# A decoder block in split fp32: the two high products of k, q, u and up become one product of 512 columns, their halves added afterwards, with PSUM handed out in single banks

## Chip, core, metric

One core of a Trainium2 chip runs the whole block in one launch. The metric is the device time of that launch in microseconds (us); the kernel before takes 1664.67 us, the median of 3 runs (1663.89 to 1665.68).

## What is computed

One layer over 256 tokens, width 2048, all in float32. Cut to the parts that matter here:

```python
h = rmsnorm(x, ln_mix)
z = h @ w_in                       # columns: u, v of the gate | q, k, v | two gates
y_a = (gelu(u) * (W_s layernorm(gelu(v)) + b)) @ w_proj_a
y_b = causal_attention(q, k, v, bias) @ w_proj_b          # 16 heads of 128
x = x + (sigmoid(g_a) * y_a + sigmoid(g_b) * y_b) @ w_out
h = rmsnorm(x, ln_mlp)
x = x + square(relu(h @ w_up)) @ w_down                   # hidden width 8192
out = rmsnorm(x, ln_final)
```

## The kernel before

Every large product has both factors split exactly into a high and a low part of type float32r, w = hi + lo and a = ah + al, and three of the four part products are summed in PSUM: ah·hi, al·hi, ah·lo.

**Weights** (`WeightStream`) come in tiles of 512 rows by 512 columns. `load` issues the DMA (raw tile, 4 buffers), `split` makes the parts: ScalarE (ACT) copies raw to `whi` (L72), VectorE (DVE) subtracts to get `wlo` (L73), 3 buffers each. `get` runs the splits two tiles ahead of the products. A *chunk* is 512 output columns over all 2048 rows, that is four weight tiles, each of four blocks kk of 128 rows.

**Products** take one of two forms. `rows` (v, the gates, the projections, w_down) has the activations as the stationary operand of 128 x 128 and 512 columns of weights moving: 24 products of 512 columns per tile. `cols` (kt, qt, u, up) gives the transposed result: the stationary operand is one of four blocks n of 128 weight columns, and 256 tokens of activations move. Per kk it runs (hi, ah) for n = 0 to 3, then (hi, al), then (lo, ah): 12 products of 256 columns, 48 per tile, 192 per chunk. There are 28 such chunks: kt, qt and u four each (kt and qt in turn, c = 0 to 3), up 16 (b = 0 to 3, c = 0 to 3). Up chunks are named up*b*_*c*.

**PSUM.** The results of `rows` and `cols` share the tag `mm` with two buffers of two banks each: one chunk fills one buffer while the chunk before is read out of the other. A chunk of `cols` holds n = 0, 1 in one bank and n = 2, 3 in the other. Its readers after the chunk are two DVE instructions of 512 columns (`scale_cols` L332, u L432, up L525), for up followed by two squares on ACT each (L527, L528) and a subtraction on DVE (L529), which make the high and low part of the hidden activations.

**Order.** The code is written in program order, and side tasks (attention heads, gating, transposes) are issued between weight tiles by `tick`. The framework then schedules every engine's instructions by its own model of durations, so that the order on an engine isn't always that of the code; on the chip an engine runs its list in that order and waits on semaphores.

Of the kernel before, what the change touches and what calls it, by code (L numbers as in the profile page):

```python
# [12 lines left out]
F32 = mybir.dt.float32  # L13
F32R = mybir.dt.float32r
# [4 lines left out]
P = 128  # L19
# [68 lines left out]
def block_kernel(ctx, tc, x, x_t, ln_mix, w_in, v_gain, w_sp, b_sp, w_pa, w_pb, w_out, rel_bias,  # L88
# [41 lines left out]

    def rows(acts, name):
        """[tokens, CH] = acts.T @ W over 2048 rows, both token tiles."""
        ps = psum.tile([P, NT, CH], F32, tag="mm", name=name, bufs=2)
        for i in range(KT // KG):
            hi, lo = stream.get()
            for kk in range(KG):
                k = i * KG + kk
                ah, al = acts(k)
                for t in range(NT):
                    s = slice(t * P, (t + 1) * P)  # L140
                    nc.tensor.matmul(ps[:, t], ah[:, s], hi[:, kk], start=k == 0, stop=False)  # L141
                    nc.tensor.matmul(ps[:, t], ah[:, s], lo[:, kk], start=False, stop=False)  # L142
                    nc.tensor.matmul(ps[:, t], al[:, s], hi[:, kk], start=False, stop=k == KT - 1)  # L143
            if i < KT // KG - 1:
                tick()
        return ps

    def cols(acts, name):
        """[CH as 4 x 128, tokens] = W.T @ acts over 2048 rows."""
        ps = psum.tile([P, CH // P, T], F32, tag="mm", name=name, bufs=2)  # L150
        for i in range(KT // KG):
            hi, lo = stream.get()
            for kk in range(KG):
                k = i * KG + kk
                ah, al = acts(k)
# [491 lines left out]
```

## Time and profile before

| what | value |
|---|---|
| median of 3 runs | 1664.67 us |
| profiled execution, its span from the first to the last instruction | 1662.5 us |
| TensorE (PE) busy | 1651.6 us, 99% of the span |
| weight loads (PEld) | 1483.7 us, 89%, beside PE |
| DVE, ACT busy | 850.9 us (51%), 688.8 us (41%) |
| read from HBM | 311.5 MB |

The profiled execution has no time of its own beside its span; the span is 2.2 us under the median of the runs, and this remainder is taken as what lies around the span. The page lists busy time by engine, the chain of work that ended last, and groups of instructions by source line. Products on PE overlap in the records (the end of one is modelled), so their rate has to be read from start to start in the timeline and not from their durations.

### The profile page before, as it was taken

The page shows a single profiled execution, that of the slowest core. Times are in us where ns is not written, and L with a number is a line of the kernel's source. Part 1 is how long each engine was busy: PE and PEld are TensorE (multiplying, and loading weights), DVE is VectorE, ACT ScalarE, POOL GpSimd, SP SyncE. Part 2 cuts the span into 40 slices and gives each one's busy share as a digit, 9 for nine tenths or more (in the row PEclk, how much of TensorE's full clock was granted, in tenths as well). Part 3 has the DMA queues.
Part 4 walks back from the last instruction along what each step waited for, and adds up shares of the span by engine and source line. Part 5 has one row for each costly group of instructions (what it writes and reads, how often), then busy time and mean ns, then how long its engine had stood idle before and what let it go on. Part 6 is the DMA issues. An engine that isn't in the chain of part 4 may idle for free.

```text
span 1662.5 us, 22670 instructions
## 1 busy us (share of the span) xinstructions
PE 1651.6 (99%) x9988; PEld 1483.7 (89%) x9988; DVE 850.9 (51%) x726; ACT 688.8 (41%) x614; POOL 4.3 (0%) x11
## 2 busy tenths in 40 slices
PE   9999999999999999999999999999999999999997
PEld 9899999888888899888888999889988998899986
DVE  7545544544445555544555555444545455445554
ACT  7444343443334443434444444334443443334432
POOL 0000000000000000000000000000000000000000
PEclk9999999999999999999999999999999999999999
DMA  9855444465555554555465554555555555555551
GB/s 317 254 193 187 165 178 170 159 223 185 200 192 189 192 199 169 184 191 202 178 234 189 210 178 178 202 189 191 178 186 194 190 190 178 201 181 186 190 183 74
DMA packets 51762, 317.16 MB, mean 191 GB/s; under 512 B 5664, under 2 KB 10832, under 8 KB 14928
## 3 DMA queue, kind: packets, MB, share of 16 engines
q1 hardware_dynamic: 51632, 315.71, 53.9%
q8 instruction: 78, 1.28, 0.3%
q14 instruction: 20, 0.16, 0.0%
q0 software_dynamic: 32, 0.01, 0.0%
HBM read 311.50 MB, written 4.19 MB: 190 GB/s over the span
## 4 chain that ended last, share of the span: by engine, by line
PE 99%; DMA 0%; DVE 0%; ACT 0%; issue 0%; DVEq 0%; POOL 0%; POOLq 0%; ACTq 0%
PE up L158 22%; PE dn L142 7%; PE dn L143 7%; PE dn L141 7%; PE kt L158 6%; PE qt L158 6%; PE u L158 6%; PE v L142 2%; PE wo L143 2%; PE ga L143 2%; PE gb L141 2%; PE wo L141 2%; PE ga L141 2%; PE wo L142 2%; PE pa L141 2%; PE v L141 2%
## 5 line engine op out<-in xcount | busy, mean ns | idle before, releaser
L73 DVE TENSOR_TENSOR wlo<-wraw,whi 128x2048 fp32r<-128x2048 f32 (+2 forms) x297 | 658.9, 2219 | 644.8 <-ACT whi L72 644.8
L72 ACT ACTIVATE whi<-wraw 128x2048 fp32r<-128x2048 f32 (+2 forms) x297 | 551.5, 1858 | 832.6 <-PE up L158 188.9
L141 PE MATMUL dn<-whi,hh 128*128 128x512 f32 x480 | 186.8, 389 | 0.0
L142 PE MATMUL dn<-wlo,hh 128*128 128x512 f32 x480 | 186.8, 389 | 0.0
L143 PE MATMUL dn<-whi,hl 128*128 128x512 f32 x480 | 186.7, 389 | 0.0
L158 PE MATMUL up<-h2h,whi 128*128 128x256 f32 x1024 | 164.7, 283 | 0.0
L158 PE MATMUL up<-h2l,whi 128*128 128x256 f32 x1024 | 164.6, 283 | 0.0
L158 PE MATMUL up<-h2h,wlo 128*128 128x256 f32 x1024 | 164.6, 283 | 0.0
L158 PEld LDWEIGHTS up<-h2h,whi 128*128 128x128 f32 x1024 | 141.5, 192 | 0.3
L158 PEld LDWEIGHTS up<-h2h,wlo 128*128 128x128 f32 x1024 | 141.3, 192 | 0.0
L158 PEld LDWEIGHTS up<-h2l,whi 128*128 128x128 f32 x1024 | 141.3, 192 | 0.0
L143 PEld LDWEIGHTS dn<-whi,hl 128*128 128x128 f32 x480 | 90.1, 188 | 18.7
L141 PEld LDWEIGHTS dn<-whi,hh 128*128 128x128 f32 x480 | 90.1, 188 | 18.6
L142 PEld LDWEIGHTS dn<-wlo,hh 128*128 128x128 f32 x480 | 90.1, 188 | 18.6
L141 PE MATMUL gb<-whi,hh 128*128 128x512 f32 x128 | 50.6, 395 | 0.0
L141 PE MATMUL wo<-whi,mh 128*128 128x512 f32 x128 | 50.6, 395 | 0.0
L141 PE MATMUL ga<-whi,hh 128*128 128x512 f32 x128 | 50.4, 394 | 0.0
L141 PE MATMUL v<-whi,hh 128*128 128x512 f32 x128 | 50.0, 391 | 0.0
L141 PE MATMUL pa<-whi,ah 128*128 128x512 f32 x128 | 50.0, 391 | 0.0
L143 PE MATMUL wo<-whi,ml 128*128 128x512 f32 x128 | 50.0, 390 | 0.0
L142 PE MATMUL v<-wlo,hh 128*128 128x512 f32 x128 | 50.0, 390 | 0.0
L143 PE MATMUL ga<-whi,hl 128*128 128x512 f32 x128 | 49.9, 390 | 0.0
(180 smaller groups left out, 2394.8 us busy)
## 6 DMA issues: line engine op xcount, KB each, us to landing
wraw<-in_w_in SPq DMA_DIRECT2D x108, 1024.0 KB, 4.8
wraw<-in_w_up SPq DMA_DIRECT2D x64, 1024.0 KB, 4.8
wraw<-in_w_down SPq DMA_DIRECT2D x64, 1024.0 KB, 4.8
wraw<-in_w_pb SPq DMA_DIRECT2D x16, 1024.0 KB, 4.8
wraw<-in_w_pa SPq DMA_DIRECT2D x16, 1024.0 KB, 4.8
wraw<-in_w_out SPq DMA_DIRECT2D x16, 1024.0 KB, 4.8
wraw<-in_w_in SPq DMA_DIRECT2D x8, 256.0 KB, 4.7
wraw<-in_w_in SPq DMA_DIRECT2D x4, 512.0 KB, 7.5
```

The source lines that it names most:

```text
L72: self.nc.scalar.activation(hi[:, s], t[:, s], AF.Copy)
L73: self.nc.vector.tensor_tensor(lo[:, s], t[:, s], hi[:, s].bitcast(F32), ALU.subtract)
L141: nc.tensor.matmul(ps[:, t], ah[:, s], hi[:, kk], start=k == 0, stop=False)
L142: nc.tensor.matmul(ps[:, t], ah[:, s], lo[:, kk], start=False, stop=False)
L143: nc.tensor.matmul(ps[:, t], al[:, s], hi[:, kk], start=False, stop=k == KT - 1)
L158: nc.tensor.matmul(ps[:, n], w[:, kk, n * P : (n + 1) * P], a, start=k == 0 and j == 0 and n % 2 == 0, stop=k == KT - 1 and j == 2, skip_g ...
```

## The change

In `cols` the high weights meet both activation parts in one product: the activations are now stored as [k][2][256], high and low side by side, and the product of the block n of `hi` with these 512 columns gives ah·hi in the first half of a bank and al·hi in the second. The low weights meet the high activations in a product of 256 columns into the first half. A block n then has a PSUM bank of its own, and the result is the sum of the two halves: `fold` copies the second half out on ACT and adds the first half on DVE. The tag `mm` has four buffers of one bank: a chunk of `cols` takes all four, `rows` takes two. In a chunk's last weight tile the products run block by block (`order`), so that the first bank is complete before the last. Scaling by the norm, which DVE did while reading PSUM, is an instruction of its own on SBUF for kt and qt (1024 columns), u (512) and up (256). All pairs of activation tiles become one tile of twice the size; docstrings and comments go.

```diff
+    def order(i, n):
+        if i == KT // KG - 1:
+            return [(kk, b) for b in range(n) for kk in range(KG)]
+        return [(kk, b) for kk in range(KG) for b in range(n)]
...
     def rows(acts, name):
-        ps = psum.tile([P, NT, CH], F32, tag="mm", name=name, bufs=2)
+        ps = [psum.tile([P, CH], F32, tag="mm", name=f"{name}t{t}", bufs=4) for t in range(NT)]
         for i in range(KT // KG):
             hi, lo = stream.get()
-            for kk in range(KG):
+            for kk, t in order(i, NT):
...
-    def cols(acts, name):
-        ps = psum.tile([P, CH // P, T], F32, tag="mm", name=name, bufs=2)
+    def cols(acts, name, finish):
+        ps = [psum.tile([P, 2, T], F32, tag="mm", name=f"{name}n{n}", bufs=4) for n in range(CH // P)]
         for i in range(KT // KG):
             hi, lo = stream.get()
-            for kk in range(KG):
+            for kk, n in order(i, CH // P):
                 k = i * KG + kk
-                ah, al = acts(k)
-                for j, (w, a) in enumerate(((hi, ah), (hi, al), (lo, ah))):
-                    for n in range(CH // P):
-                        nc.tensor.matmul(ps[:, n], w[:, kk, n * P : (n + 1) * P], a,
-                                         start=k == 0 and j == 0 and n % 2 == 0,
-                                         stop=k == KT - 1 and j == 2, skip_group_check=True)
+                a, s = acts(k), slice(n * P, (n + 1) * P)
+                nc.tensor.matmul(ps[n], hi[:, kk, s], a, start=k == 0, stop=False, skip_group_check=True)
+                nc.tensor.matmul(ps[n][:, 0], lo[:, kk, s], a[:, 0], start=False, stop=k == KT - 1,
+                                 skip_group_check=True)
...
-        return ps
+        for n in range(CH // P):
+            finish(n, ps[n])
+
+    def fold(dst, ps):
+        nc.scalar.activation(dst, ps[:, 1], AF.Copy)
+        nc.vector.tensor_tensor(dst, ps[:, 0], dst, ALU.add)
...
+        def scale(dst):
+            nc.vector.tensor_tensor(dst, dst, rb[1][:, None, :].to_broadcast([P, 4, T]), ALU.mult)
+        def summed(name):
             dst = at.tile([P, 4, T], F32, tag=name[:2], name=name, bufs=2)
+            cols(hacts, name, lambda n, ps: fold(dst[:, n], ps))
             return dst
         for c in range(4):
-            ps = cols(hacts, f"kt{c}")
-            kt = scale_cols(ps, f"kt{c}") if c else None
+            kt = summed(f"kt{c}")
...
-            pq = cols(hacts, f"qt{c}")
-            kt = kt or scale_cols(ps, f"kt{c}")
-            qt = scale_cols(pq, f"qt{c}")
+            qt = summed(f"qt{c}")
+            scale(kt)
+            scale(qt)
...
+            def finish_u(n, ps, uc=uc):
+                fold(uc[:, n], ps)
+                if n % 2:
+                    s = slice(n - 1, n + 1)
+                    nc.vector.tensor_tensor(uc[:, s], uc[:, s], rb[1][:, None, :].to_broadcast([P, 2, T]),
+                                            ALU.mult)
+                    nc.scalar.activation(uc[:, s], uc[:, s], AF.Gelu)
...
+            def finish_up(n, ps, hd=hd):
+                v = mlp.tile([P, T], F32, tag="v", name="v", bufs=2)
+                q = mlp.tile([P, T], F32, tag="q", name="q", bufs=2)
+                fold(v, ps)
+                nc.vector.scalar_tensor_tensor(v, v, 0.0, rb[2], op0=ALU.max, op1=ALU.mult)
+                nc.scalar.activation(hd[:, n, 0], v, AF.Square)
                 nc.scalar.activation(q, v, AF.Square)
-                nc.vector.tensor_tensor(tl[:, s], q, th[:, s].bitcast(F32), ALU.subtract)
+                nc.vector.tensor_tensor(hd[:, n, 1], q, hd[:, n, 0].bitcast(F32), ALU.subtract)
```

Three places in the order of instructions. The names: whi164 and wlo164 are the parts of weight tile 164, the first of chunk up0_1; up0_1n2 is the PSUM bank of its block n = 2; a chunk without an n is the kernel before.

PE, from the end of chunk up0_0 to the first tile of up0_1, before:

```order
L158 MATMUL up0_0_7056<-h2l_6468,whi163_7133 128x256 x3
L158 MATMUL up0_0_7056<-h2h_6467,wlo163_7134 128x256 x4
L158 MATMUL up0_1_7325<-h2h_6467,whi164_7205 128x256 x4
L158 MATMUL up0_1_7325<-h2l_6468,whi164_7205 128x256 x4
L158 MATMUL up0_1_7325<-h2h_6467,wlo164_7206 128x256 x4
```

PE, in the first tile of up0_1, after; six products of n = 0 and 1 stand ahead of these rows and three blocks kk of them ahead of the first of n = 2:

```order
L162 MATMUL up0_1n0_6662<-h2_5842,wlo164_6556 128x256
L161 MATMUL up0_1n1_6663<-h2_5842,whi164_6555 128x512
L161 MATMUL up0_1n2_6664<-h2_5842,whi164_6555 128x512 [waits DVE_49]
L162 MATMUL up0_1n2_6664<-h2_5842,wlo164_6556 128x256
L161 MATMUL up0_1n2_6664<-h2_5842,whi164_6555 128x512
L161 MATMUL up0_1n3_6665<-h2_5842,whi164_6555 128x512 [waits DVE_49]
```

Before, the new chunk waits for no bank; after, its blocks 2 and 3 wait for DVE and stand behind three blocks kk of n = 0 and 1.

DVE, at the end of chunk up0_1 (weight tiles 164 to 167; 168 to 171 are up0_2), before:

```order
L73 TENSOR_TENSOR wlo169_7491<-wraw169_7326,whi169_7490 128x2048 [waits DMAHW0_49,PE_49,Activation_49]
L525 SCALAR_TENSOR_TENSOR v_7544<-up0_1_7325,rb2_7192 128x512 [waits PE_49]
L525 SCALAR_TENSOR_TENSOR v_7550<-up0_1_7325,rb2_7192 128x512
L73 TENSOR_TENSOR wlo170_7560<-wraw170_7380,whi170_7559 128x2048 [waits DMAHW1_49,Activation_49]
L529 TENSOR_TENSOR hl0_1_7543<-q_7545,hh0_1_7542 128x512 [waits Activation_49]
```

DVE, at the same place, after:

```order
L73 TENSOR_TENSOR wlo169_6783<-wraw169_6666,whi169_6782 128x2048 [waits DMAHW0_49,PE_49,Activation_49]
L171 TENSOR_TENSOR v_6818<-up0_1n0_6662,v_6818 128x256 [waits Activation_49]
L171 TENSOR_TENSOR v_6826<-up0_1n1_6663,v_6826 128x256 [waits Activation_49]
L531 SCALAR_TENSOR_TENSOR v_6818<-v_6818,rb2_6542 128x256 [waits DVE_49]
L531 SCALAR_TENSOR_TENSOR v_6826<-v_6826,rb2_6542 128x256 [waits DVE_49]
L534 TENSOR_TENSOR hd0_1_6661<-q_6819,hd0_1_6661 128x256 [waits Activation_49]
L534 TENSOR_TENSOR hd0_1_6661<-q_6827,hd0_1_6661 128x256 [waits Activation_49]
L171 TENSOR_TENSOR v_6834<-up0_1n2_6664,v_6834 128x256 [waits DVE_49,Activation_49]
L171 TENSOR_TENSOR v_6842<-up0_1n3_6665,v_6842 128x256 [waits DVE_49,Activation_49]
```

The adds that free banks 2 and 3 stand behind the whole treatment of blocks 0 and 1, which goes to ACT and back. At the ends of kt, qt (c = 1 to 3) and u the three adds of n = 0 to 2 follow each other and the fourth stands behind the next `wlo`; on PE the first tile of the next chunk then runs n = 0 to 2 through all four kk (11 or 12 pairs) before n = 3.

DVE, around the end of the first chunk kt0 (weight tiles 0 to 3), before; the two scalings of kt0, which read its banks, come 14 rows after these and qt0 fills the other buffer meanwhile:

```order
L281 COPY rv_190<-rvp_509 16x384 [waits PE_49]
L73 TENSOR_TENSOR wlo4_316<-wraw4_197,whi4_315 128x1024 [waits DMAHW2_49,Activation_49]
L73 TENSOR_TENSOR wlo4_316<-wraw4_197,whi4_315 128x1024 [waits Activation_49]
L239 TENSOR_TENSOR sq_97<-sq_97 128x512 [waits DVE_49]
L282 MEMSET rv_190 16x128 [waits DVE_49]
```

DVE, at the same place, after:

```order
L288 COPY rv_188<-rvp_442 16x384 [waits PE_49]
L73 TENSOR_TENSOR wlo4_286<-wraw4_199,whi4_285 128x1024 [waits DMAHW2_49,Activation_49]
L73 TENSOR_TENSOR wlo4_286<-wraw4_199,whi4_285 128x1024 [waits Activation_49]
L171 TENSOR_TENSOR kt0_194<-kt0n0_195,kt0_194 128x256 [waits Activation_49]
L171 TENSOR_TENSOR kt0_194<-kt0n1_196,kt0_194 128x256 [waits Activation_49]
L73 TENSOR_TENSOR wlo5_327<-wraw5_201,whi5_326 128x1024 [waits DMAHW3_49,Activation_49]
```

The adds of kt0 now stand right behind both halves of wlo4, and qt0 can't start before the first of them has read its bank.

## Rows read from the trace of the kernel before

**Rows 1.** The page: span, busy time by engine, the chain that ended last.
```profile
span 1662.5 us, 22670 instructions
PE 1651.6 (99%) x9988; PEld 1483.7 (89%) x9988; DVE 850.9 (51%) x726; ACT 688.8 (41%) x614; POOL 4.3 (0%) x11
PE 99%; DMA 0%; DVE 0%; ACT 0%; issue 0%; DVEq 0%; POOL 0%; POOLq 0%; ACTq 0%
```

**Rows 2.** Stretches, one in up: busy us and count by engine, granted clock, DMA share, GB/s.
```profile
1000.00:1200.00 200.00, 200.00 (x1327) 185.01 (x1327) 100.11 (x64) 78.44 (x56) 0.00 (x0) 1.00 0.53 188
```

**Rows 3.** Timeline of PE, from chunk up0_3 to dn: start, us, instruction, count.
```profile
1005.09 0.64 PE L158 MATMUL up<-h2h,whi 128*128 128x256 f32 x4
1005.57 0.64 PE L158 MATMUL up<-h2l,whi 128*128 128x256 f32 x4
...
1027.65 0.64 PE L158 MATMUL up<-h2h,wlo 128*128 128x256 f32 x4
1028.13 0.40 PE L141 MATMUL dn<-whi,hh 128*128 128x512 f32 x1
...
1029.52 0.39 PE L141 MATMUL dn<-whi,hh 128*128 128x512 f32 x1
```

**Rows 4.** Timeline of all engines in wo, products of 512 columns.
```profile
904.46 0.39 PE L141 MATMUL wo<-whi,mh 128*128 128x512 f32 x1
...
906.27 0.39 PE L143 MATMUL wo<-whi,ml 128*128 128x512 f32 x1
...
906.75 1.92 ACT L72 ACTIVATE whi<-wraw 128x2048 fp32r<-128x2048 f32 x1 [0.78 <-PE wo L143]
...
911.26 0.39 PE L141 MATMUL wo<-whi,mh 128*128 128x512 f32 x1
```

**Rows 5.** Timeline near the end, products of 256 columns in the form of `rows`.
```profile
1643.73 0.28 PE L574 MATMUL last<-whi,hh 128*128 128x256 f32 x1
...
1647.34 0.40 PE L574 MATMUL last<-spare,hh 128*128 128x256 f32 x2
```

**Rows 6.** Groups by line and shape: count, busy us, mean ns, idle before.
```profile
L158 PE MATMUL up<-h2l,whi 128*128 128x256 f32 x1024 | 164.6, 283 | 0.0
L158 PE MATMUL qt<-hl,whi 128*128 128x256 f32 x256 | 41.4, 283 | 0.0
L158 PE MATMUL u<-hl,whi 128*128 128x256 f32 x256 | 41.1, 283 | 0.0
L158 PE MATMUL kt<-hl,whi 128*128 128x256 f32 x256 | 41.1, 283 | 0.0
L323 ACT ACTIVATE bh<-pv 128x256 fp32r<-128x256 f32 x16 | 5.1, 373 | 0.0
L324 DVE TENSOR_TENSOR bl<-pv,bh 128x256 fp32r<-128x256 f32 x16 | 6.0, 416 | 0.0
L303 DVE SCALAR_TENSOR_TENSOR l<-sc,bt 128x256 f32<-128x256 f32 x16 | 6.6, 413 | 0.0
```

**Rows 7.** Timeline of ACT and DVE around the start of chunk up0_3.
```profile
1004.81 1.91 ACT L72 ACTIVATE whi<-wraw 128x2048 fp32r<-128x2048 f32 x1 [3.85 <-PE up L158]
1005.29 1.29 DVE L525 SCALAR_TENSOR_TENSOR v<-up,rb 128x512 f32<-128x512 f32 x2 [2.00 <-PE up L158]
1006.63 0.61 ACT L527 ACTIVATE hh<-v 128x512 fp32r<-128x512 f32 x1
1006.75 2.29 DVE L73 TENSOR_TENSOR wlo<-wraw,whi 128x2048 fp32r<-128x2048 f32 x1 [0.18 <-ACT whi L72]
1008.97 1.28 DVE L529 TENSOR_TENSOR hl<-q,hh 128x512 fp32r<-128x512 f32 x2
```

**Rows 8.** The chain that ended last, pieces: start, us, what.
```profile
30.17 2.28 PE qt L158 x19
...
83.67 0.66 PE ptp L316 x6
```

**Rows 9.** Timeline of DVE at the end of kt0.
```profile
28.89 2.34 DVE L73 TENSOR_TENSOR wlo<-wraw,whi 128x1024 fp32r<-128x1024 f32 x2
```

**Rows 10.** Timeline of ACT and of PE in chunk v0.
```profile
62.69 1.92 ACT L72 ACTIVATE whi<-wraw 128x2048 fp32r<-128x2048 f32 x1 [12.45 <-DMA wraw<-in_w_in]
...
66.40 0.58 PE L141 MATMUL v<-whi,hh 128*128 128x512 f32 x1
66.98 0.50 PE L142 MATMUL v<-wlo,hh 128*128 128x512 f32 x1
```

More of the change, by code (lines that the diff above doesn't have):

```diff
@@ L182, in block_kernel @@
     ab = ab_open.enter_context(tc.tile_pool(name="ab", bufs=1))
-    xt = ab.tile([P, KT, T], F32, tag="ab", name="xt", bufs=2)
-    sq = ab.tile([P, KT, T], F32, tag="ab", name="sq", bufs=2)
+    both = ab.tile([P, 2, KT, T], F32, tag="ab", name="xt", bufs=1)
+    xt, sq = both[:, 0], both[:, 1]
     first = [((0, 1), (1, 2), (2, 3), (3, 4))] * 2 + [((0, 2), (2, 4))] * 2
@@ L264, in transpose_pair @@
         return tp
-    bh = bl = None
+    bp = None
     with tc.tile_pool(name="attn", bufs=1) as at:
@@ L438, in block_kernel @@
         for c in range(4):
-            ps = rows(lambda k: (ah[:, k], al[:, k]), f"pa{c}")
+            ps = rows(lambda k: ap[:, k], f"pa{c}")
             for t in range(NT):
-                nc.scalar.activation(pa[:, t, c * CH : (c + 1) * CH], ps[:, t], AF.Copy)
-        mh = ab.tile([P, KT, T], F32R, tag="ab", name="mh", bufs=2)
-        ml = ab.tile([P, KT, T], F32R, tag="ab", name="ml", bufs=2)
+                nc.scalar.activation(pa[:, t, c * CH : (c + 1) * CH], ps[t], AF.Copy)
+        mp = ab.tile([P, KT, 2, T], F32R, tag="ab", name="mp", bufs=1)
         def merged(c):
@@ L500, in block_kernel @@
     for c in range(4):
-        ps = rows(lambda k: (mh[:, k], ml[:, k]), f"wo{c}")
+        ps = rows(lambda k: mp[:, k], f"wo{c}")
         for t in range(NT):
-            add_rows(ps[:, t], t, slice(c * CH, (c + 1) * CH), ssq2[:, t, c : c + 1])
+            add_rows(ps[t], t, slice(c * CH, (c + 1) * CH), ssq2[:, t, c : c + 1])
         if c == 3:
@@ L537, in block_kernel @@
                 if last:
-                    add_rows(ps[:, t], t, s, ssq3[:, t, c : c + 1])
+                    add_rows(ps[t], t, s, ssq3[:, t, c : c + 1])
                     nc.vector.tensor_tensor(x1[:, t, s], x1[:, t, s], lnf[:, s], ALU.mult)
                 else:
-                    add_rows(ps[:, t], t, s)
-    spare = [hold.tile([P, KG, CH], F32R, tag="h", name=f"spare{i}", bufs=2) for i in range(2)]
-    stream.spare = tuple(spare)
+                    add_rows(ps[t], t, s)
+    spare = hold.tile([P, 2, KG, CH], F32R, tag="h", name="spare", bufs=1)
+    stream.spare = (spare[:, 0], spare[:, 1])
     out_v = out.rearrange("(t p) d -> t p d", p=P)
@@ L571, in product @@
             hi, lo = parts[k // KG]
-            ah, al = acts(k)
+            pair = acts(k)
+            ah, al = pair[:, 0], pair[:, 1]
             for j, (x_, w_) in enumerate(((ah, hi), (ah, lo), (al, hi))):
@@ L578, in block_kernel @@
     c0, half = D - CH, CH // 2
-    ps = psum.tile([P, NT, CH], F32, tag="mm", name="last", bufs=2)
-    product(ps[:, 0], 0, parts, 0, CH)
-    finish(ps[:, 0], 0, c0, D, 3)
+    ps = psum.tile([P, CH], F32, tag="mm", name="last", bufs=4)
+    product(ps, 0, parts, 0, CH)
+    finish(ps, 0, c0, D, 3)
     last_norm(0)
-    product(ps[:, 1, :half], 1, parts, 0, half)
-    finish(ps[:, 1, :half], 1, c0, c0 + half, 3)
+    ps = psum.tile([P, half], F32, tag="mm", name="last1", bufs=4)
+    product(ps, 1, parts, 0, half)
+    finish(ps, 1, c0, c0 + half, 3)
     ps = psum.tile([P, half], F32, tag="tp", name="last2", bufs=2)
```

90 lines of the change are left out of this document (33 added, 57 removed).

## Prediction

> **What bounds the kernel now.** The page was read first. PE is busy for 99% of the span and the chain of work that ended last is 99% PE [rows 1], so only PE's own time and new waits of PE can move the end; DVE and ACT, at 51% and 41%, have room. The stretches come next: in up PE shows no idle time in 200 us, and the granted clock is 1.00, the upper level of 2.4 GHz [rows 2]. The cost of a product therefore has to be read from start to start. The fourth and last chunk of a block of up runs from 1005.09 to 1028.13 us [rows 3]: 23.04 us for 192 products of 256 columns, 120.0 ns each. A tile of wo, in the form of `rows`, has 30 starts of 512 columns between 904.46 and 911.26 us [rows 4]: 226.7 ns each. The step of 106.7 ns is 256 columns at 2.4 GHz, so 13.3 ns are left in both widths that do not grow with the columns. The products of `last` have 256 columns but the roles of the operands that `rows` has; 30 intervals from 1643.73 to 1647.34 us [rows 5] give 120.3 ns. The 13.3 ns thus go with the product, and neither with the form nor with which operand stands still.
>
> **The change part by part.** *Products.* Per kk, 12 products of 256 columns become 4 of 512 and 4 of 256. The columns stay at 3072; four products go. The groups of al·hi have 1024 entries for up and 256 each for kt, qt and u [rows 6], 1792 in all, and 1792 x 13.3 ns = 23.9 us leave PE's path. A chunk falls from 23.04 to 64 x (226.7 + 120.0) ns = 22.19 us. No trace of before has the two widths in turn. If one product of each of the 1792 pairs hid its constant behind the other width, or paid it twice, the saving would be 47.8 us or nothing; since three stretches with two widths and two roles give the same 13.3 ns [rows 3 to 5], I take that value and leave the lower end to a rival.
>
> *Start.* kt0 and qt0 should each gain 0.85 us. Before, qt0 starts at 30.17 us [rows 8] with no bank to wait for. After, its first product needs the first add of kt0, which stands on DVE behind both halves of wlo4, and DVE works on those from 28.89 for 2.34 us [rows 9]. So qt0 starts at 28.89 + 2.34 + 0.42 (an add, by the 256-column reading of PSUM on DVE [rows 6]) = 31.65 us, 1.5 us later. What PE gains after that is lost again at v0: there ACT waits 12.45 us for a weight tile by DMA, splits it from 62.69 us on, and the low products follow at 66.98 behind a product that stretches to 0.58 us [rows 10]. The tile's arrival is set by the DMA queue, which nothing in the change makes faster, so time is pinned there whether qt0 started early or late. I take 2.0 us of the 23.9 as lost: kt0's and qt0's 1.7 us and a little of kt1. Bounds: 0 if the loads move with the products, 3.5 us if qt0's delay also pushes the request of later tiles.
>
> *Fold.* 112 copies on ACT at about 0.373 us and 112 adds on DVE at about 0.416 us [rows 6] are 42 and 47 us of new work, on engines with over 800 us of idle time each [rows 1]; the squares and subtractions are split into halves, at a little more than their old time. They cost nothing unless a bank is given back late. Its cover is therefore the time between the end of a block and the first product of the next chunk that wants the same bank.
>
> *Banks, up to up* (12 places). Set t = 0 at the first product of a chunk's last tile; a block takes 4 x 0.347 = 1.39 us and the tile 5.55. ACT starts a `whi` 0.48 us after the last high product that read its buffer [rows 4], at about 0.1 here, for 1.92 us, then copies n0 and n1. DVE makes `wlo` from 2.1 to 4.3: 2.2 us from its start to the next instruction [rows 7]. Adds of n0 and n1 end at 5.0, the two maxima at 5.7, squares on ACT at 6.6, two subtractions at 7.1, and the adds of n2 and n3 at 7.4 and 7.7. PE comes to n2 of the next chunk after six products and pairs of n0 and n1, at 5.55 + 1.96 = 7.51, and to n3 at 8.08. No wait, by 0.1 us. With full durations in place of intervals the add of n2 ends at 8.06 and PE loses 0.55 us, 6.6 us over the twelve. I take the intervals, since DVE's pair at 1005.29 and the one at 1008.97 lie on its path at 0.65 us apiece [rows 7].
>
> *Banks, kt to qt and u to u* (7 places). The fourth add stands behind another `wlo`: copy of n3 until 7.9, `wlo` 7.6 to 9.8, add until 10.3. PE comes to n3 at 5.55 + 0.66 (the transposes of ptp [rows 8]) + 4.04 = 10.25, in u at about 10.5. That is 0.05 us of waiting, 0.5 at the worst: 3.5 us over seven. At the four ends of up to dn, and where `rows` and `cols` change places elsewhere, `rows` takes two banks, and the other two come free long before they are wanted.
>
> *Shared PSUM.* After the end of up0_3, six dn products start between 1028.13 and 1029.52 us [rows 3], 231.7 ns against 226.7, while DVE reads PSUM. More and shorter reads could stretch more products: 5 ns for two to three products at each of 27 ends is 0.35 us, 2.8 us at most if all the copies and adds do it. For these three places together, waits and stretching, I take 1.2 us of 0 to 13.
>
> **Sum.** -23.9 + 2.0 + 1.2 = -20.7 us. The profiled span of 1662.5 us [rows 1] becomes 1641.8. The span stands 2.2 us under the median of the runs, 1664.67, and that remainder is kept: 1644.0 us.
>
> **The rivals.** *The forecast* (0.71): 1640 to 1648, by the bounds of start and stretching and by waits of 0 to 0.2 us at a transition.
>
> *Waits at the banks* (0.18): the chains above have a margin of 0.1 us. A DMA that arrives late, or a `wlo` that stands 0.4 us later than in my chain, puts 0.3 to 1 us on each of the 19 transitions, 6 to 19 us: 1648 to 1661, still faster. For it speaks that DVE has 2.2 us `wlo` instructions [rows 7] that an add may have to sit behind; against it that PE has filled the gap with blocks of n0 and n1.
>
> *The constant does not go with the product* (0.05). If the two widths in turn cost more than their rates say, so that a pair pays the constant three times and the time goes by columns alone, the 53 ns (4 x 13.3) saved per kk come back and the time is 1664.7 + 1.2 + 0 to 1 us: 1665 to 1667, no difference. Rows 3 to 5 speak against it. The Trainium skill, page "TensorE: Matmul & The Clock Gate", section "Back-to-back issue gap", bears on this: it puts the gap at the columns over 2.4 GHz and about 2.5 ns. By that figure four removed products would be worth an estimated 1792 x 2.5 ns = 4.5 us and the time would come to about 1662; this trace has 13.3 ns where the page has 2.5, so the rows decide.
>
> *Slower: banks without fill-in* (0.06). If PE reached n3 of the next chunk in the order of the code, it would want it in the first kk, at 5.55 + 1.04 = 6.59, and the seven transitions with the late add would each lose 10.3 - 6.6 = 3.7 us, 26 us; the twelve of up would want n2 at 6.24 and get it at 7.4, 1.2 us each, 14 us. The 40 us exceed the gain: 1664.7 - 20.7 - 1.2 + 40, about 1683. It decides from (23.9 - 2.0)/19 = 1.15 us a transition. Against it stands the order of PE's instructions, in which n2 and n3 follow after several kk of n0 and n1; the same could come about if these fill-in products themselves wait, for n0's own add or for weights that DVE splits late because of the adds.
>
> **How the numbers follow.** The likeliest is the forecast, 1644.0. Forecast and bank waits are both faster: 0.89. No difference, within 0.2% or 3.3 us, which is about what a measurement of this kernel can tell: 0.05, and slower 0.06. The range goes from 1639, all bounds favourable, to 1653, which takes in a little under half of the bank waits.
>
> **What the changed profile would show.** In the middle of a chunk of up a pair of a 512-column and a 256-column product should take 0.347 us and a whole chunk some 22.2 us; PE's busy time falls by 22 to 24 us with no idle time of note. The first products of n2 and n3 in a chunk wait under 0.1 us for DVE's add (L171). qt0 starts at 31.6 us, and the low product of v0 still starts at about 67 us. DVE and ACT each show 112 more instructions and about 40 to 50 us more. I am wrong on the gain if the pair does not take 0.347 us; on the banks, if PE's idle time ahead of L161 ended by DVE exceeds 3 us in sum; on the start, if the low product of v0 comes 1.5 us earlier or later than 67.

## The result, and the profile after

The changed kernel takes 1650.24 us (median of 4 runs, 1649.82 to 1650.81) against 1664.28 us for the kernel before beside it: a ratio of 0.9912, interval 0.9898 to 0.9926. That is 14.0 us faster, in the range and on the side that was forecast, but short of the 20.7 us of the sum: the span falls by 14.4 us (1662.5 to 1648.1), 6.3 us less than forecast. The time also lies outside the 1640 to 1648 us that the prediction gave for the forecast itself; the range takes it in by its upper part, which was made for the rival of waits at the banks.

The page of the changed kernel:

```profile
span 1648.1 us, 19486 instructions
PE 1635.4 (99%) x8196; PEld 1386.6 (84%) x8196; DVE 895.3 (54%) x894; ACT 731.9 (44%) x790; POOL 4.2 (0%) x11
```

Against [rows 1], exactly the 1792 products are gone, and DVE and ACT have 44 and 43 us more to do, as worked out, in 168 and 176 more instructions and not 112, since squares, maxima and subtractions were split as well. PE is busy for 99% of the span as before, but its busy time falls by 16.2 us where 22 to 24 were forecast. What is new shows only where whole chunks are set side by side. Stretches of the changed kernel, the four chunks of block 1 of up and one of block 0 (columns as in [rows 2]):

```profile
1108.26:1130.87 22.61, 22.61 (x130) 19.59 (x128) 11.19 (x9) 8.62 (x7) 0.00 (x0) 1.00 0.55 189
1130.87:1153.11 22.24, 22.24 (x130) 19.56 (x129) 13.25 (x17) 11.21 (x17) 0.00 (x0) 1.00 0.53 190
1153.11:1175.45 22.34, 22.34 (x131) 19.55 (x130) 13.37 (x17) 11.32 (x17) 0.00 (x0) 1.00 0.51 186
1175.45:1197.78 22.33, 22.33 (x131) 19.54 (x129) 13.36 (x17) 11.35 (x17) 0.00 (x0) 1.00 0.55 191
954.13:976.51 22.38, 22.38 (x130) 19.53 (x129) 13.40 (x17) 11.36 (x17) 0.00 (x0) 1.00 0.54 188
```

The forecast had 22.19 us for each. up1_1 comes close, but up1_0, the first row, takes 22.61 with the same products, no wait, less work on DVE and ACT beside it, and the same granted clock of 1.00. PE's timeline of the changed kernel, a piece of that slow chunk and a piece of up1_3:

```profile
1110.73 0.40 PE L161 MATMUL up_0n<-h,whi 128*128 128x512 f32 x1
1110.96 0.28 PE L162 MATMUL up_0n<-h,wlo 128*128 128x256 f32 x1
1111.08 0.40 PE L161 MATMUL up_0n<-h,whi 128*128 128x512 f32 x1
...
1112.14 0.40 PE L161 MATMUL up_0n<-h,whi 128*128 128x512 f32 x1
...
1179.75 0.39 PE L161 MATMUL up_3n<-h,whi 128*128 128x512 f32 x1
...
1181.14 0.39 PE L161 MATMUL up_3n<-h,whi 128*128 128x512 f32 x1
```

From 1110.73 to 1112.14 and from 1179.75 to 1181.14 lie four pairs each: about 353 ns a pair in the slow chunk and 347 in the other, and PE's starts to the nanosecond give 353.3 and 346.7 over the whole of each. The pair that the sum rests on exists at two rates.

Where the 23.9 us of 1792 x 13.3 ns went, by the starts of PE's products in the two traces:

| stretch (us) | before | after | gained, of the count's share | share not gained |
|---|---|---|---|---|
| start of kt1 | 77.76 | 78.62 | -0.86 of 1.71 | 2.6 |
| kt1 to the end of v3 (six chunks changed) | 222.87 | 220.01 | 2.86 of 5.12 | 2.3 |
| u (four) | 97.44 | 95.35 | 2.09 of 3.41 | 1.3 |
| up, block 0 | 93.46 | 90.59 | 2.87 of 3.41 | 0.5 |
| up, blocks 1 to 3, each | 92.15 | 89.52 | 2.63 of 3.41 | 0.8 |
| after the last product starts | 9.06 | 9.54 | -0.48 of 0 | 0.5 |

All other stretches agree to 0.1 us. Sorted by kind, from kt1 on: intervals that exceed their nominal width by less than 25 ns, thus the slow pairs, add up to 3.7 us more than before; longer ones, waits at banks and first products after a task, to 2.4 us; 0.3 is in the products of the tasks. With the 2.6 us before kt1 and the 0.5 at the end these make up the 9.5 us between the 23.9 and the 14.4.

Who waited for the adds of the changed kernel (line L171; engine, waiting group, us in all, times):

```profile
  PEld qt0n L161: 1.6, 1
  PE qt0n L161: 1.3, 1
  PEld up_2n L161: 0.8, 4
  PEld up_3n L161: 0.8, 4
  PEld up_1n L161: 0.2, 1
  PEld qt1n L161: 0.2, 1
```

After the start each wait is 0.2 us on the queue of weight loads, 14 of them with qt2, qt3, u2 and u3: 2.8 us, only in part PE's own.

### The profile page after: what moved, and what is told of

It is laid out like the page before. It is cut to its first block, busy times and chain, and to the rows that moved or that the text cites. A ratio compares the mean times of both kernels' runs of the same rounds, so it can differ in the third digit from the quotient of the medians.

```text
span 1648.1 us, 19486 instructions
## 1 busy us (share of the span) xinstructions
PE 1635.4 (99%) x8196; PEld 1386.6 (84%) x8196; DVE 895.3 (54%) x894; ACT 731.9 (44%) x790; POOL 4.2 (0%) x11
## 4 chain that ended last, share of the span: by engine, by line
PE 97%; DVE 1%; DMA 1%; ACT 0%; SPq 0%; issue 0%; DVEq 0%; ACTq 0%
PE up_0n L161 4%; PE up_2n L161 4%; PE up_3n L161 4%; PE up_1n L161 4%; PE up_1n L162 2%; PE up_3n L162 2%; PE up_2n L162 2%; PE up_0n L162 2%; PE dn_0t L146 2%; PE dn_0t L147 2%; PE dn_2t L146 2%; PE dn_2t L145 2%; PE dn_1t L146 2%; PE dn_1t L147 2%; PE dn_0t L145 2%; PE dn_1t L145 2%
## 5 line engine op out<-in xcount | busy, mean ns | idle before, releaser
L161 PE MATMUL up_0n<-h,whi 128*128 128x512 f32 x256 | 90.5, 398 | 0.0
L161 PE MATMUL up_2n<-h,whi 128*128 128x512 f32 x256 | 88.9, 393 | 0.0
L161 PE MATMUL up_3n<-h,whi 128*128 128x512 f32 x256 | 88.9, 393 | 0.0
L161 PE MATMUL up_1n<-h,whi 128*128 128x512 f32 x256 | 88.7, 392 | 0.0
L162 PE MATMUL up_0n<-h,wlo 128*128 128x256 f32 x256 | 71.7, 280 | 0.0
L162 PE MATMUL up_1n<-h,wlo 128*128 128x256 f32 x256 | 70.4, 280 | 0.0
L162 PE MATMUL up_2n<-h,wlo 128*128 128x256 f32 x256 | 70.4, 280 | 0.0
L162 PE MATMUL up_3n<-h,wlo 128*128 128x256 f32 x256 | 70.4, 280 | 0.0
L147 PE MATMUL dn_0t<-whi,hd 128*128 128x512 f32 x128 | 49.9, 390 | 0.0
L145 PE MATMUL dn_0t<-whi,hd 128*128 128x512 f32 x128 | 49.8, 389 | 0.0
L145 PE MATMUL dn_1t<-whi,hd 128*128 128x512 f32 x128 | 49.8, 389 | 0.0
L147 PE MATMUL dn_1t<-whi,hd 128*128 128x512 f32 x128 | 49.8, 389 | 0.0
```

Source lines behind the costliest of these rows:

```text
L145: nc.tensor.matmul(ps[t], a[:, 0, s], hi[:, kk], start=k == 0, stop=False)
L147: nc.tensor.matmul(ps[t], a[:, 1, s], hi[:, kk], start=False, stop=k == KT - 1)
L161: nc.tensor.matmul(ps[n], hi[:, kk, s], a, start=k == 0, stop=False, skip_group_check=True)
L162: nc.tensor.matmul(ps[n][:, 0], lo[:, kk, s], a[:, 0], start=False, stop=k == KT - 1, skip_group_check=True)
```

## The experiments

The changed kernel and the twelve kernels of the experiments, each against the kernel before on its own chip; kt1 and the rest of the span are from one profile of each. The intervals reach some 2 us to either side, so most of these kernels can't be told from the changed one by their times; where they differ by less, the argument rests on chunks within the profiles.

| run | ratio to before | interval | start of kt1 | kt1 to the end of the span |
|---|---|---|---|---|
| before | 1 | | 77.76 | 1584.76 |
| changed kernel | 0.9912 | 0.9898 to 0.9926 | 78.62 | 1569.50 |
| groups of four | 0.9936 | 0.9923 to 0.9948 | 82.93 | 1571.63 |
| one swap | 0.9916 | 0.9903 to 0.9930 | 79.78 | 1569.58 |
| two halves | 1.0024 | 1.0015 to 1.0033 | 81.03 | 1586.38 |
| up only | 0.9930 | 0.9916 to 0.9943 | 77.40 | 1573.71 |
| swap after rows | 0.9921 | 0.9908 to 0.9933 | 79.89 | 1570.79 |
| sixteen | 0.9928 | 0.9914 to 0.9941 | 81.22 | 1569.48 |
| groups of two | 0.9931 | 0.9913 to 0.9950 | 81.68 | 1569.55 |
| fold on DVE | 0.9976 | 0.9966 to 0.9986 | 84.66 | 1573.81 |
| kt0 freed by ACT | 0.9924 | 0.9911 to 0.9936 | 79.46 | 1569.87 |
| up freed by ACT | 0.9930 | 0.9917 to 0.9942 | 78.31 | 1572.37 |
| sixteen, freed by ACT | 0.9970 | 0.9958 to 0.9982 | 86.51 | 1570.11 |
| first two old | 0.9907 | 0.9890 to 0.9924 | 79.98 | 1569.25 |

**Two halves: does the gain go with the number of products?**

```diff
-                nc.tensor.matmul(ps[n], hi[:, kk, s], a, start=k == 0, ...)
+                nc.tensor.matmul(ps[n][:, 0], hi[:, kk, s], a[:, 0], start=k == 0, ...)
+                nc.tensor.matmul(ps[n][:, 1], hi[:, kk, s], a[:, 1], start=False, ...)
```

> The changed kernel, but each product of 512 columns is two products of 256, the high and the low activations apart, into the two halves of the same bank; banks, folds and order stay. PE runs 192 products in a chunk again. Theory, 13.3 ns go with each product: 1792 x 13.3 ns = 23.9 us come back, less some 3 us of the slow alternation that then cannot happen, 1671; and since this is the kernel before but for banks, folds and start, the difference to 1664.3, 6 to 7 us, is the price of these alone. Rival, the time goes by columns and the gain came from elsewhere in the change (order, banks): 1650 to 1652.

Measured: 1669.38 us, 0.24% slower than before (the interval leaves out 1). The first theory holds, with banks and folds cheaper than the 6 to 7 us expected. A stretch of this kernel, the first chunk of block 1 and the first products of the next:

```profile
1119.63:1142.70 23.07, 23.07 (x194) 23.07 (x193) 11.18 (x9) 8.76 (x8) 0.00 (x0) 1.00 0.53 187
```

With the changed kernel's banks and folds the chunk is back at 23.03 us by PE's starts, 120.0 ns a product. Banks and folds alone cost 1.6 us from kt1 to the end (1586.38 against 1584.76) and some 3 us at the start. The joint product is worth 19.3 us of span (1667.4 to 1648.1) where the count promised 23.9; the slow pairs' 3.7 us are most of the difference. Every product has its own weight load in all of these kernels, so that the runs do not tell whether the 13.3 ns belong to the product or to its load.

**Up only: do the parts add up?** kt, qt and u keep the old `cols` and its scaling from PSUM:

```diff
-            qt = summed(f"qt{c}")
+            pq = old_cols(hacts, f"qt{c}")
+            qt = scale_cols(pq, f"qt{c}")
```

> The change for up alone: kt, qt and u have the three products of 256 columns and the scaling from PSUM of the kernel before, in two of the four single banks; up has the product of 512 columns and the fold. By the two traces, up's 16 chunks should gain 13.65 us and lose 3.3 (0.54 us in block 0, 0.78 in each of the others), and kt, qt and u should gain 10.2 and lose 6.1, of which 2.6 at the start. Theory, the parts add up and the start is lost to the fold of kt0: 1664.3 - 10.3 + 0.4 (end of the span) = 1654.4, kt1 starting at 77.8 us as before and not at 78.6. Rival, the loss at the start comes from the banks or from the joint activation tile: kt1 starts late here too and the time is 1655 or more.

Measured: 1653.28 us. The parts add up and the start is as before, as in the theory. The old chunks cost what they did: kt1 at 77.40, and 587.09 us from kt1 to the end of u against 587.10. From there to the end of the span the kernel is 11.0 us faster than before. The changed kernel's 14.4 us of span thus split into some 10 to 11 for up (of 13.7) and 4 for kt, qt and u together (of 10.2).

**Is the slow pair a matter of the order?** First the widths in groups of four, four and four per kk:

```diff
+            for g in range(0, len(pairs), 4):
+                for low in (False, True):
+                    for kk, n in pairs[g : g + 4]:
...
```

> The changed kernel, but per kk the four products of 512 columns run first and the four of 256 after them (in a chunk's last weight tile the four kk of a block likewise), so that the two widths no longer alternate. In the changed kernel the alternating pairs run at two rates, 346.7 ns a pair in most chunks of up and 353.3 ns in u0, in up_0 of the later blocks and in qt1 to qt3, some 63 pairs x 6.6 ns = 0.42 us a chunk. Theory 1, the slow rate is a state that the strict alternation of widths can fall into: with groups of four every chunk runs at 1386.7 ns per kk, nothing of the 353.3 is left, and the time is 1650.2 - 3 = 1647. Rival, the slow rate belongs to the place (chunks that follow rows or attention work, with DVE and ACT reading PSUM or other transfers beside them): the same chunks stay 0.4 us long and the time is 1650.

Measured: 1654.06 us. PE's timeline of this kernel, one kk in up1_0:

```profile
1117.20 0.64 PE L165 MATMUL up_0n<-h,wlo 128*128 128x256 f32 x4
1117.67 1.09 PE L168 MATMUL up_0n<-h,whi 128*128 128x512 f32 x4
1118.60 0.63 PE L165 MATMUL up_0n<-h,wlo 128*128 128x256 f32 x4
```

A kk takes 1118.60 - 1117.20 = 1.40 us, 1.403 in the mean of ten, and not 1.387: the first theory is refuted, and so is its rival, since a kk now costs the same in up_0 and in its neighbours. Breaking the strict alternation does not by itself give the better rate; two changes of width per kk cost 17 ns. The remaining loss, up to kt1 at 82.93, is the start, below. Groups of two, the same with 2 in place of 4:

```diff
+            for g in range(0, len(pairs), 2):
```

> The changed kernel in groups of two high and two low products (4 changes of width per kk, where groups of four have 2 and the alternation 8). If a change of width costs 6.6 ns, a kk takes 1387 + 4 x 6.6 = 1413 ns in the middle of a chunk; if the cost is one of the whole group (13 ns per group of high and low), it takes 1387 + 2 x 13 = 1413 too, and if only the state of the alternation counts, 1387 or 1400. The time follows from it: 28 chunks x 16 kk x 26 ns = 12 us over the 1639 of no loss, 1655 with the other losses of 4 us, against 1645 for no cost.

Measured: 1653.35 us, from two runs alone. By PE's starts a kk in the middle of up1_0 takes 1.393 us there, none of the values expected. More changes of width do not cost more, so there is no price of 6.6 ns for each change.

Then one exchange at the start of each chunk, the rest alternating:

```diff
+            steps = [(kk, n, low) for kk, n in pairs for low in (False, True)]
+            if i == 0:
+                steps[1], steps[2] = steps[2], steps[1]
...
```

> The changed kernel with one edit in the order of PE: at the start of each chunk of k, q, u and up the first low product and the second high product change places (high, high, low, low), and everything after alternates as in the changed kernel. Theory 1, how the alternation begins decides its rate for the whole chunk: up_0 of the later blocks and u0, now at 353.3 ns a pair with nothing to disturb them, change their rate, to 346.7 if a break of the alternation is what ends the slow state; then 4 x 0.42 = 1.7 us go and the time is 1648.5. Rival, the rate belongs to the place of the chunk: 353.3 ns stays there and the time is 1650.2.

Measured: 1651.06 us. Stretches of this kernel, up1_0 to up1_2:

```profile
1108.98:1131.18 22.20, 22.20 (x129) 19.40 (x128) 11.08 (x9) 8.50 (x7) 0.00 (x0) 1.00 0.56 192
1131.18:1153.87 22.69, 22.69 (x130) 19.59 (x129) 13.46 (x17) 11.41 (x17) 0.00 (x0) 1.00 0.52 186
1153.87:1176.44 22.57, 22.57 (x130) 19.59 (x129) 13.35 (x17) 11.31 (x17) 0.00 (x0) 1.00 0.52 187
```

up1_0 fell from 22.61 to 22.20, as the first theory had it, and its neighbours rose from 22.24 and 22.34 to 22.69 and 22.57; the time stayed (1569.58 us from kt1 on against 1569.50). So the place does not decide the rate. With the exchange only in u0 and up_0, where it had helped:

```diff
-            if i == 0:
+            if i == 0 and (name == "u0" or name[:2] == "up" and name[-1] == "0"):
```

> The changed kernel with the swap of the earlier run (high, high, low, low as the first four products) only in u0 and in up_0 of each block, the chunks that follow a chunk of 512-column products. In that run up_0 of the later blocks took 22.20 us instead of 22.61, but up_1 and up_2, which had run at 346.7 ns a pair, were swapped too and fell to 353.2. Theory 1, the beginning decides the rate of the alternation: up_0 and u0 stay at 347 ns and up_1 to up_3 keep the 346.7 ns of the changed kernel, 4 x 0.42 = 1.7 us less: ratio to the changed kernel 0.999, 1648.5. Rival, the rates of the chunks of a block are bound to one another (one of the four has to be slow, up_1 takes over what up_0 is spared): 1650.

Measured: 1651.38 us. Two pairs of stretches of this kernel, up1_2 and up1_3, then up3_1 and up3_2, none of them exchanged:

```profile
1155.15:1177.84 22.69, 22.69 (x131) 19.61 (x129) 13.47 (x17) 11.42 (x17) 0.00 (x0) 1.00 0.53 186
1177.84:1200.09 22.25, 22.25 (x130) 19.57 (x129) 13.24 (x17) 11.27 (x17) 0.00 (x0) 1.00 0.53 190
...
1485.91:1508.61 22.70, 22.70 (x131) 19.61 (x129) 13.47 (x17) 11.43 (x17) 0.00 (x0) 1.00 0.54 186
1508.61:1530.86 22.25, 22.25 (x131) 19.57 (x129) 13.24 (x16) 11.21 (x17) 0.00 (x0) 1.00 0.51 186
```

up_0 of blocks 1 to 3 stayed at the better rate, but u0 was at the other in spite of the exchange, and so were one or two chunks of each block that had been well before: up_2 is slow in block 1 and not in block 3. Blocks 1 to 3 run up's products in the same order. Theory and rival fall both: the order does not fix the rate. Up only and first two old say the same: up's products of blocks 1 to 3 have there the very order of the changed kernel, and up_0 takes 22.20 us in all three blocks instead of 22.61, with no neighbour slow in its place.

Last, all 16 wide products of a tile ahead of its 16 narrow ones:

```diff
+            groups = [[(kk, n) for n in range(CH // P) for kk in range(KG)]]
...
```

> The changed kernel with all 16 products of 512 columns of a weight tile ahead of its 16 of 256 (block by block; in a chunk's last tile 4 and 4 for each block, so that banks are completed one by one). With groups of four a kk took 1400 ns in place of 4 x 346.7 = 1387, 6.6 ns for each change of width. Theory 1, each change of width may cost up to half of the 13.3 ns and only a fortunate alternation avoids it: with 2 changes a tile (8 in the last) a chunk has 14 x 6.6 = 0.09 us over the 22.19, against 0.42 in the slow chunks now, and the tasks between tiles cost what they did; kt1 to the end falls by some 3 us and the time is 1647, or 1649 if the start loses time at v0 again as with groups of four, where tiles came late (kt1 at 82.9 us). Rival, longer runs of 512 columns cost something of their own, or n2's bank is wanted earlier than it is free: 1651 or more.

Measured: 1652.80 us, where the theory had 1647 to 1649. Stretches of this kernel, up1_0 and up1_1:

```profile
1110.34:1132.63 22.29, 22.29 (x130) 19.66 (x129) 12.31 (x12) 10.42 (x12) 0.00 (x0) 1.00 0.60 216
1132.63:1155.09 22.46, 22.46 (x131) 19.57 (x130) 13.76 (x17) 11.65 (x17) 0.00 (x0) 1.00 0.52 186
```

up_0 takes 22.29 us in blocks 1 to 3 alike, 0.10 over the 22.19, which is what the theory expected; up_1 to up_3 lose 0.3 each to waits at n3 and the products around them, as the rival has it. From kt1 to the end this equals the changed kernel (1569.48 and 1569.50), and the difference in time is the start (kt1 at 81.22).

**The banks.** A fold in one DVE instruction:

```diff
-        nc.scalar.activation(dst, ps[:, 1], AF.Copy)
-        nc.vector.tensor_tensor(dst, ps[:, 0], dst, ALU.add)
+        nc.vector.tensor_reduce(dst, ps.rearrange("p h t -> p t h"), axis=mybir.AxisListType.X, op=ALU.add)
```

> The changed kernel with a fold that is one DVE instruction: a sum of the two halves read from the bank, without ACT's copy. It takes ACT and the hand-over out of the way of the bank's release and 42 us off ACT, and makes DVE's instruction longer (512 values in place of 256, about 0.65 us by DVE's 512-column readings of PSUM). Theory, waits at the banks cost 1.7 us after the start (that is what the run with two halves loses to the kernel before from kt1 on) and are set by ACT's copy behind a whi: half or more of them go, and qt0 starts no later: 1649 to 1650. Rival, DVE is what holds the banks: its longer instructions add 0.25 us to each of four folds ahead of the next, 0.5 to 1 us at the 19 chunk ends, 1655 to 1665.

Measured: 1661.17 us, the time of the rival. A group of this kernel by line and shape:

```profile
L170 DVE TENSOR_REDUCE v<-up_1n 128x256 f32<-128x512 f32 x16 | 11.0, 685 | 11.6 <-PE up_1n L162 11.6
```

685 ns against 416 for the add: up_1 to up_3 take 0.3 to 0.6 us more than 22.19, and from kt1 on the kernel loses 4.3 us against the changed one. That part is of the rival's kind, though far under its 0.5 to 1 us at each of 19 chunk ends; the other 6.0 us lie ahead of kt1 (84.66), where the rival had nothing: PE waits 3.1 us in v0 for parts of weight tiles that are split late. Then ACT alone frees the banks of up:

```diff
-                v = mlp.tile([P, T], F32, tag="v", name="v", bufs=2)
+                w = mlp.tile([P, 2, T], F32, tag="v", name="v", bufs=4)
+                v = w[:, 0]
...
-                fold(v, ps)
+                nc.scalar.activation(w, ps, AF.Copy)
+                nc.vector.tensor_tensor(v, v, w[:, 1], ALU.add)
```

> The changed kernel with the same way of folding in up alone: ACT copies the whole bank, DVE adds from SBUF. ACT gets 64 longer copies (about 0.24 us each, 15 us in all, beside PE). In the changed kernel up_1 to up_3 lose 0.04 to 0.2 us each at n2 and n3, and up_0 of the later blocks 0.42 us to the slow alternation. Theory, DVE's adds hold the banks: the waits go, 12 x 0.15 = 1.8 us at most, and the time is 1648.5 to 1649; a chunk may change its rate of alternation either way, 0.42 us each. Rival, ACT's copies stand behind a whi of 1.9 us and the first products of n2 wait for ACT, as long as they did for DVE or longer: 1650 to 1653.

Measured: 1652.75 us, within the rival's times but not by its waits. A stretch of this kernel, up0_1, to set beside 22.38 us of the changed kernel:

```profile
954.74:977.39 22.65, 22.65 (x130) 19.59 (x129) 13.69 (x18) 12.33 (x17) 0.00 (x0) 1.00 0.52 189
```

Its waits at n2 and n3 are nearly gone in block 0, and the chunk is 0.27 us longer: nearly all of it runs at the slow pair now. In up as a whole the slow pairs rose by 2.5 us, and waits with what follows them fell by 0.45. This fits the finding that no chunk gained by losing its wait: a wait ends one run of alternating products, and the next runs at either rate.

**The start.** ACT alone frees the banks of kt0, and of kt0 only:

```diff
+                def fold0(n, ps):
+                    w = whole[n // 2][:, n % 2]
+                    nc.scalar.activation(w, ps, AF.Copy)
+                    nc.vector.tensor_tensor(dst[:, n], w[:, 0], w[:, 1], ALU.add)
```

> The changed kernel with kt0 alone folded in another way: ACT copies each whole bank (512 columns) to SBUF and DVE adds the halves there, so that kt0's banks come free by ACT and no longer by the adds behind wlo4. In the changed kernel qt0 starts at 31.49 us, 1.46 us after kt0's last product, and kt1 at 78.62 (before: 77.76). Theory, that wait is what the start loses most and PE has no stall behind it up to kt1: qt0 starts within 0.2 us of kt0's end, kt1 at 77.2 to 77.8, and the time falls by 0.8 to 1.4 us to about 1649.2. Rival, the second half of v0 is pinned by its weight tile (low product at 67 us, as the prediction has it): qt0 starts early, but v0 waits for it and kt1 stays at 78.4 to 78.7: 1650.2.

Measured: 1651.76 us, no gain. The wait of qt0 is gone, and PE then waits in v0. PE's timeline of this kernel:

```profile
67.21 0.81 PE L145 MATMUL v0t<-whi,hp 128*128 128x512 f32 x2
68.90 0.50 PE L146 MATMUL v0t<-wlo,hp 128*128 128x512 f32 x1 [0.87 <-DVE wlo L73]
```

This is the rival's mechanism, a weight tile that pins v0, though not at its number. On the queue of weight tiles (SP) the table of attention biases is written to HBM (rv_d) and read back (bt), and the tile comes behind that. Timelines of SP and ACT, the changed kernel and then this one:

```profile
35.47 0.69 SPq L292 DMA_DIRECT2D rv_d<-rv  x1
60.02 0.39 SPq L299 DMA_DIRECT2D bt<-rv_d  x1
62.87 1.92 ACT L72 ACTIVATE whi<-wraw 128x2048 fp32r<-128x2048 f32 x1 [6.83 <-DMA wraw<-in_w_in]
...
36.86 0.69 SPq L292 DMA_DIRECT2D rv_d<-rv  x1
61.72 0.39 SPq L299 DMA_DIRECT2D bt<-rv_d  x1
64.60 1.92 ACT L72 ACTIVATE whi<-wraw 128x2048 fp32r<-128x2048 f32 x1 [8.85 <-DMA wraw<-in_w_in]
```

The table goes out 1.39 us later here and the tile is split 1.73 us later. In the profiles of the kernel before, the changed kernel and all experiments but the one that moves the first bias to another queue, this split begins 27.4 to 28.6 us after the table goes out: at 62.16 us in up only (table at 34.26), at 66.38 to 68.19 with groups of four and of two, the sixteens and the fold on DVE (table at 38.22 to 40.72), where PE waits 0.8 to 3.1 us in v0. With the sixteens, groups of four and the fold on DVE v0 takes 26.2 to 28.3 us against 23.2 in the changed kernel, which is most of their late kt1. What sent the table out late in each was not varied by itself. The start also moves without it: the same old chunk kt0 takes 24.12 us in up only and 26.59 in first two old, so that one profile each does not settle a microsecond there.

The same kernel holds the clearest evidence on the pair. Stretches, up1_0 and up2_0:

```profile
1109.74:1131.94 22.20, 22.20 (x129) 19.41 (x128) 11.07 (x9) 8.52 (x7) 0.00 (x0) 1.00 0.54 190
1286.06:1308.67 22.61, 22.61 (x130) 19.59 (x128) 11.19 (x9) 8.62 (x7) 0.00 (x0) 1.00 0.53 189
```

The same products in the same order, the chunks behind them and the instructions of DVE and ACT beside them too, in one execution: 0.41 us apart. By PE's starts the two begin alike (227, 113, 233, 117 and 241 ns from one product to the next); the next interval is 119 ns in the first chunk and 127 in the second, and there the rates part.

The sixteens, kt0 and up freed by ACT, and the first attention bias moved to the POOL queue:

```diff
-            nc.sync.dma_start(bt, rv_d[4 * c : 4 * c + 4]...)
+            (nc.sync if c else nc.gpsimd).dma_start(bt, rv_d[4 * c : 4 * c + 4]...)
```

> Together: 16 products of 512 columns and then 16 of 256 per weight tile, banks of kt0 and of up freed by ACT, and the first attention bias fetched through the POOL queue, so that SP's queue of weight tiles doesn't stand behind it from 52 to 60 us. From kt1 to the end the run of sixteens took 1569.5 us, of which 0.28 us in each of 12 chunks of up is waits and slow products behind them, against 0.10 in up_0 of the later blocks. Theory, these 0.18 x 12 = 2.2 us and the stall of 1.8 us in v0 go: kt1 at 77.8, end of the span at 1645.1, time 1647, the best so far. Rival, tiles arrive no earlier and v0 stalls as before (kt1 at 81): 1650 or more.

Measured: 1659.46 us, worse than each of the three kernels that it joins. DVE's timeline of this kernel:

```profile
70.41 0.29 DVE L317 SCALAR_TENSOR_TENSOR l<-sc,bt 128x128 f32<-128x128 f32 x1 [13.51 <-DMA bt<-rv_d]
...
72.00 2.28 DVE L73 TENSOR_TENSOR wlo<-wraw,whi 128x2048 fp32r<-128x2048 f32 x1
```

The bias came later, DVE stood 13.5 us before the row that adds it, and `wlo` of v0 stood behind that row, so that PE waited 6.9 us in v0. So the time says nothing for or against the sixteens. From kt1 on the run does: 1570.11 us against 1569.48 for the sixteens alone, with up_1 to up_3 at 22.52 us instead of 22.46 to 22.49, so the 2.2 us that freeing up's banks by ACT was to bring are not there.

Last, kt0 and qt0 in the old form and all else changed:

```diff
+            if c:
+                qt = summed(f"qt{c}")
+            else:
+                pq = old_cols(hacts, f"qt{c}")
```

> The changed kernel with the first two chunks, kt0 and qt0, left in the old form: three products of 256 columns per block and kk, two banks each, scaled on DVE once the norm is there; all other chunks of k, q, u and up as changed. In the run with up alone, where these two chunks are old as well, kt1 started at 77.40 us; in the changed kernel at 78.62, behind the wait of 1.46 us for kt0's fold and a second tile of v0 that its loads allow at about 67 us. Theory, the new form loses at the start what it gains and more, because the fold of kt0 delays qt0 and the row of biases on DVE: kt1 at 77.3 to 77.8 us, everything after as in the changed kernel (1569.5 us to the end), end of the span at 1647.1, time 1649.2 on the chip of the prediction, ratio to the kernel before 0.9905 to 0.991. Rival, start and rest are not separate (the rates of alternation after kt1 fall otherwise, or kt1 starts at 78.5 or later): 1650 to 1652.

Measured: 1649.36 us, ratio 0.9907. The point estimate is the best of all, but the interval takes in the changed kernel's 0.9912. In the profiled execution, which took 1650.93 us where the others took 1649.02 to 1649.64, kt0 waited 2.3 us in all for the splits of the first tiles, so kt1 at 79.98 does not show the start that was expected; the rest, 1569.25 us, is as in the changed kernel. Whether the old form is better there stays open.

## Why the prediction was right, and where it was too large

*The bound and the mechanism* were right: PE's own time moves the end, 13.3 ns go with each product, and the two halves bring most of the 23.9 us back. That the time lies in the range is in part luck: it is outside the 1640 to 1648 us of the forecast, and the range reaches further for a rival that did not come about.

*The step that failed is the size of the gain.* The prediction said that no trace of before has the two widths in turn, named 47.8 us and nothing as the ends, and then wrote "I take that value and leave the lower end to a rival"; that rival loses the whole gain, and a pair between the two had no term in the sum. In turn the pair costs 346.7 or 353.3 ns. 6.6 ns over a chunk of 64 pairs is 0.42 us, half of its gain. In the changed kernel's profile u0, up_0 of three blocks, most of qt and parts of kt were at the upper of the two: 3.7 us. Of the 6.3 us of span between the sum and the result 3.7 are these pairs, 1.5 waits and task products beyond the 1.2 taken, 0.6 the start beyond the 2.0, and 0.5 the end. The sign that the prediction set itself, a pair that does not take 0.347 us, came about in these chunks. A term "0 to 0.42 us in each of 28 chunks" would have put the middle at 1650.

*The rule of the Trainium skill* that the prediction set beside the rows ("TensorE: Matmul & The Clock Gate", section "Back-to-back issue gap", 2.5 ns a product) is given there for an isolated product, and not for a stream of weight loads and products, which the prediction left out. By that figure the joint product would have been worth an estimated 4.5 us. The two halves against the changed kernel show 19.3 us, so the figure does not carry over to this stream.

*Banks.* Taken at 1.2 us; the two halves, where nothing alternates, lose 1.6 us from kt1 on. Right in kind and nearly in size: 0.2 us on the weight loads at each of 14 places, where under 0.1 was forecast, and not one longer. PE's fill-in of n0 and n1 is the likely reason; no run takes it away. The rival of 0.3 to 1 us at every transition, whose time of 1648 to 1661 would have fitted the result, is not what happened; the largest part of the shortfall comes from inside the chunks. The slower rival, banks without fill-in, never came up.

*Start.* qt0 at 31.49 us for the forecast 31.65, with the add behind both halves of wlo4 as named. (Before, it starts at 30.01 us by PE's starts; the 30.17 of [rows 8] is where a piece of the chain begins.) Taken at 2.0 us lost, it is 2.6, but not by the path of the prediction: 1.5 are qt0's wait for the add, 0.3 a later first product, 0.5 each a smaller gain in kt0 and in qt0, and v0 wins 0.2 back. PE's timeline of the changed kernel:

```profile
31.49 0.51 PE L161 MATMUL qt0n<-hp,whi 128*128 128x512 f32 x1 [1.30 <-DVE kt L171]
...
67.50 0.81 PE L145 MATMUL v0t<-whi,hp 128*128 128x512 f32 x2
68.15 0.40 PE L146 MATMUL v0t<-wlo,hp 128*128 128x512 f32 x1
```

The low product of v0, forecast "at about 67 us", starts at 68.15 without a wait, because PE itself comes later; the tile was there in time. The pin exists, as the run with kt0 freed by ACT shows, but it lies beside PE's own arrival and not ahead of it, and it isn't fixed: the tile follows the bias table on SP's queue.

*The end.* The 0.5 us after the last product were not in the sum. DVE and ACT rows there are the same to 0.02 us until the stores; what is left lies in these, 3.1 us from issue to landing in the median against 2.7. It belongs to the change: the stretch after the last product starts takes 9.06 us before and 9.07 in two halves, 9.38 in up only, and 9.53 to 9.58 in the changed kernel and the ten others. Why the stores take longer stays open.

## What to carry to other kernels

When products are merged to save their fixed cost, measure that cost in the mixture that will run, not only in streams of one width: here the mixture of 512 and 256 columns cost up to half of the saving. Compare equal chunks of one trace with each other before explaining a loss by waits; here a loss with no idle time and no wait was seen only there. And a wait taken out of a kernel that is bound by such a stream may return as pace.

## What the runs showed of the hardware that was not expected

Strictly alternating products of 512 and 256 columns, each with its own weight load, settle at 346.7 or 353.3 ns a pair and stay there for tens of pairs, at a granted clock of 1.00. At the slow rate of up1_0 in the changed kernel the starts repeat in threes: the wide products' intervals are 232, 236 and 240 ns, a third of them each, and three pairs take 1060 ns; in up1_3 every wide interval is 230 ns and three pairs take 1040. The same code ran at both rates within one run (22.20 and 22.61 us). The rate was seen to change at a task between two weight tiles, in either direction (in the changed kernel kt3 goes from 347 to 353 ns a pair there, u1 from 353 to 347), and to settle within the first few pairs of a chunk. An exchange of two products at a chunk's start and a wait that was gone went with other rates in later chunks too. In groups of two a kk cost 1.393 us, in groups of four 1.403, against 1.387 and 1.413 for the two rates of the alternation; streams of one width showed only 226.7 and 120.0 ns. What sets the rate was not found: the order of products, the place in the kernel and the work of DVE and ACT were each held equal with the rate different, and DMA was busy 0.52 to 0.55 of the time in the slow stretches of up and 0.51 to 0.57 in the others.
